# Small fp32 products in places of the array, and the inverse moved out of the chain, in a one-layer gMLP and RWKV-7 step

## The chip, the core and the metric

The kernel runs on one core of one Trainium2 chip, in one launch. The metric is device time in microseconds (us). An execution before the change took 1997.01 us (median of three, 1996.12 to 1997.17).

## The reference

One layer of a hybrid trunk takes 1024 prompt frames and 64 sample frames of width 2048, in fp32. Its core, cut:

```
z = rms_norm(x) @ w_in                       # 2048 -> 7296 columns
u, v, g_a | r, k, v_b, hw, ha | g_b = z      # the second group is token-shifted
out_a = gelu(u) * (tril(W_s) @ layer_norm(gelu(v)) + b_s) * silu(g_a)
w = exp(-exp(-softplus(-(w0 + tanh(hw) @ w2)) - 0.5));  a = sigmoid(a0 + ha @ a2)
kk = normalise_per_head(k * k_k);  k = k * (1 + (a - 1) * k_a)
for each t:                                  # 16 heads of 64, state S is 64 x 64
    S = S * w_t + (-S @ kk_t) (kk_t * a_t)^T + v_t k_t^T
    y_t = S @ r_t
out_b = (group_norm(y) + (r.k.r_k per head) * v) * silu(g_b)
y = rms_norm(x + [out_a ; out_b] @ w_out)
```

## The kernel before, in words

**Projections.** Both large products run in f16. Each fp32 operand is split by a power-of-two scale into a high and a low half, and three passes (high by high, high by low, low by high) stand for one fp32 product. The input projection is cut into 57 blocks of 128 columns. Each block runs over three groups of frames (364, 364 and 360), with 16 k-tiles of three passes in each. These products write the tile mp from the h operands, which lie in `big` (bigt in the profile), and the weight halves w. The out-projection is cut into two halves of the mixed columns, and within each into eight groups of 256 output columns; it reads the mixed operands from mixT. Operand j of a half is a tile of 128 columns by 1088 frames. `mix_stage` (L1169) reads it from DRAM into a buffer, and `mix_prep` (L1131) makes its high half on ACT and its low half on DVE. `out_first` (L1203) is the first group: for a tile of 128 frames it runs over operands 0 to 5 first, then 6 and 7. In the kernel before, the first three operands are placed in the tile hw and two buffers of the keys, and the other five in u buffers as these come free.

**The RWKV part.** It runs beside the input projection and the first out-projection half, one pair of heads q at a time, in 16 chunks of 64 frames plus the sample's chunk 16. For each pair:

- `front(q)` (L771) makes decay, a, the normalised keys and the scaled operands AR (from kk and r) and KB (from b and k). It sums squares over each head with a 128x128 block matrix of ones, `bones`, and it does so again for the bonus.
- `wkv(q)` (L867) makes the masked products of each chunk in MK: MA (for the delta rule) and MR (for the output). The side generator `ktr` transposes KB for the state update. Then it inverts a unit triangular matrix per chunk and head: 32x32 blocks by DVE steps, and the block between them by two batches of 32x32 products on TensorE (L953 to L971).
- MA holds two blocks per chunk and head: the inverse, and the block that multiplies the values. The products L982 to L991 apply the second to the values; POOL then clears it, so that what is left of MA is the inverse of both heads on its diagonal.
- The chain (L996 to L1048) then goes from chunk to chunk: a product of AR with the state S into yps, the sum with the values into `sar` on DVE, the product of the inverse with sar (L1006), two copies of the result into VS, the product of the transposed keys with VS, and the new state on DVE. After every fourth chunk, four products of MR with VS give the output y.

**What sets the order.** The program text emits one instruction list, in the order in which a planner in Python runs. `mm` (L221) adds an estimate to the clock of TensorE. Every two or three f16 products, `poll` (L151) lets each waiting side generator whose time has come emit its next piece. So the fp32 products stand between f16 products, where the planner expects their inputs to be there. A piece that emits several products without a `yield` puts them directly one behind another. Small products write PSUM tiles from two pools with two buffers each: `bigt` (bigp in the profile) and `smt` (smp). A product that reuses a buffer waits until the buffer's reader, mostly ACT, is through.

Engines are named as in the profile: PE is TensorE, ACT is ScalarE, DVE is VectorE, POOL is GpSimd, SP issues DMAs.

## Time and profile before

| | |
|---|---|
| median of three runs | 1997.01 us |
| profiled execution, its own time | 1997.49 us |
| span of its instructions | 1995.4 us |
| PE busy | 1948.3 us, 98% |
| DVE busy | 1295.7 us, 65% |
| ACT busy | 967.5 us, 48% |
| POOL busy | 351.4 us, 18% |
| mean granted clock of TensorE | 0.993 |
| HBM traffic | 91 GB/s over the span |

Busy time of an engine is the time in which it has an instruction under way. Products on TensorE are pipelined, and the end of one is modelled, so its duration runs into the start of the next; the time from one start to the next is what a product takes from the engine. An fp32 product shows as two instructions. The span leaves out about 2 us around the first and last instruction, which the execution's time holds.

### The profile page before, as it was taken

Reading aid. Unit: us, or ns where it says so; the run is one execution under the profiler, and the core shown is the slowest. Engines: PE = TensorE matmul, PEld = TensorE weight load, DVE = VectorE, ACT = ScalarE, POOL = GpSimd, SP = SyncE. Lnnn points to the kernel's source line nnn. Section 1 sums busy time; section 2 is a strip of 40 time slices with the busy share of each in tenths; the row PEclk is TensorE's granted clock in tenths of the full one; section 3 lists DMA queues with packets and bytes.
Section 4 is the critical chain, followed back from the end, with each engine's and each line's share of the span. In section 5 each row is a group of like instructions: output and inputs, shape, how many; then the busy total and the mean of one; then the engine's idle time right before and its main releaser. Section 6 shows DMA issues by size and latency. Waiting matters only on the chain. (4 is left out here: it accounts for less than half of the span.)

```text
span 1995.4 us, 40192 instructions
## 1 busy us (share of the span) xinstructions
PE 1948.3 (98%) x16709; PEld 1421.8 (71%) x16709; DVE 1295.7 (65%) x3173; ACT 967.5 (48%) x1702; POOL 351.4 (18%) x352
## 2 busy tenths in 40 slices
PE   6999999999999999999999999999999899999998
PEld 6966667656766666676676677667667578889997
DVE  6584684494686667667667765956766686663444
ACT  7642352536455544744555564374465524242433
POOL 2500002500420330041023023004202401000000
PEclk8999999999999999999999999999999999999999
DMA  6221114121212212312321231222222353142114
GB/s 237 86 75 43 46 66 171 67 76 70 88 63 99 85 58 77 122 56 80 100 100 48 77 123 58 77 92 87 79 90 99 144 193 109 35 156 97 74 43 139
DMA packets 49301, 183.79 MB, mean 92 GB/s; under 512 B 6560, under 2 KB 18352, under 8 KB 39456
## 3 DMA queue, kind: packets, MB, share of 16 engines
q1 hardware_dynamic: 39792, 150.02, 21.0%
q0 software_dynamic: 6880, 22.26, 3.2%
q10 hardware_dynamic: 2448, 8.94, 1.1%
q8 instruction: 132, 2.16, 0.4%
q14 instruction: 49, 0.40, 0.1%
HBM read 135.86 MB, written 45.38 MB: 91 GB/s over the span
## 5 line engine op out<-in xcount | busy, mean ns | idle before, releaser
L231 PE MATMUL mp<-bigt,w 128*128 128x364 f16 (+3 forms) x8496 | 1337.7, 310 | 2.2 <-DVE w L190 1.4
L231 PEld LDWEIGHTS <-w 128*128 128x128 f16 x9216 | 821.1, 99 | 409.0 <-issue 16.3
L190 DVE SCALAR_TENSOR_TENSOR w<-raw,sci,w 128x512 f16<-128x512 f32 x276 | 220.6, 814 | 87.7 <-ACT w L182 86.0
L231 PEld LDWEIGHTS <-wk 128*128 128x128 f16 x2304 | 210.0, 98 | 28.9 <-DVE wk L190 4.8
L182 ACT ACTIVATE w<-raw,sci 128x512 f16<-128x512 f32 x276 | 186.3, 713 | 68.2 <-DVE sci L268 65.1
L231 PE MATMUL mp<-w,wk 128*128 128x256 f16 x1728 | 205.6, 273 | 4.2 <-DVE wk L190 4.2
L194 POOL TENSOR_TENSOR u<-u,u 128x1088 f32<-128x1088 f32 x56 | 138.0, 2475 | 288.1 <-DVE u L190 207.1
L182 ACT ACTIVATE w<-raw 128x2048 bf16<-128x2048 f32 (+1 forms) x70 | 131.8, 1883 | 81.2 <-PE mp L231 76.5
L182 ACT ACTIVATE wk<-bigp 128x512 f32<-128x512 f32 (+5 forms) x200 | 94.3, 492 | 123.0 <-PE bigp L231 88.9
L214 DVE STREAM_TRANSPOSE wk<-u 32x288 f32<-32x288 f32 (+1 forms) x256 | 115.8, 452 | 52.0 <-ACT u L182 47.5
L182 ACT ACTIVATE u<-mp,sc 128x364 f32<-128x364 f32 (+3 forms) x109 | 57.1, 524 | 183.8 <-PE mp L231 182.8
L231 PE MATMUL mp<-w,u 128*128 128x256 f16 x960 | 122.6, 275 | 6.7 <-DVE u L190 6.7
L182 ACT ACTIVATE u<-mp,zs 128x364 f32<-128x364 f32 (+1 forms) x75 | 42.0, 560 | 166.9 <-PE mp L231 162.5
L182 ACT ACT_TABLE_LOAD x91 | 116.8, 1283 | 9.9 <-PE bigp L231 6.0
L190 DVE SCALAR_TENSOR_TENSOR S<-S,pc,smp 64x64 f32<-64x64 f32 x240 | 66.9, 279 | 70.0 <-PE smp L231 68.1
L190 DVE SCALAR_TENSOR_TENSOR bigt<-mp,sc,bigt 128x512 f32<-128x512 f32 (+2 forms) x83 | 54.0, 652 | 86.9 <-PE mp L231 86.4
L231 PEld LDWEIGHTS <-u 128*128 128x128 f16 x960 | 94.0, 99 | 20.1 <-DVE u L190 8.0
L990 POOL MEMSET wk<- 64x512 f32 (+1 forms) x48 | 18.9, 395 | 500.2 <-PE bigp L231 498.7
L194 POOL TENSOR_TENSOR wk<-wk,mask 128x512 f32<-128x512 f32 (+1 forms) x80 | 83.1, 1058 | 130.5 <-ACT wk L182 119.8
L182 ACT ACTIVATE u<-yps 64x128 f32<-64x128 f32 x120 | 32.7, 272 | 143.0 <-DVE sar L194 134.4
L231 PE MATMUL bigp<-wk 64*128 64x128 f32 (+2 forms) x1360 | 99.6, 259 | 0.0
L231 PEld LDWEIGHTS bigp<-wk 64*128 64x128 f32 (+2 forms) x1360 | 85.3, 167 | 18.9 <-issue 9.4
(179 smaller groups left out, 2087.9 us busy)
## 6 DMA issues: line engine op xcount, KB each, us to landing
raw<-w_in SPq DMA_DIRECT2D x54, 1024.0 KB, 4.8
raw<-w_out SPq DMA_DIRECT2D x14, 1024.0 KB, 4.9
z_d<-u SPq DMA_DIRECT2D x24, 544.0 KB, 2.9
u<-z_d SPq DMA_DIRECT2D x24, 544.0 KB, 5.5
mix_d<-u ACTq DMA_DIRECT2D x16, 544.0 KB, 2.7
u<-mix_d POOLq DMA_DIRECT2D x16, 544.0 KB, 5.5
o_y<-bigt SPq DMA_DIRECT2D x16, 512.0 KB, 4.0
wk<-x SPq DMA_DIRECT2D x7, 1024.0 KB, 7.7
```

The source lines that it names most:

```text
L182: self.nc.scalar.activation(out, in_, func, bias=bias, scale=scale, **kw)
L190: self.nc.vector.scalar_tensor_tensor(out, in0, s, in1, op0, op1)
L194: (eng or self.nc.vector).tensor_tensor(out, a, b, op)
L214: self.nc.vector.transpose(out, a)
L231: self.nc.tensor.matmul(out, lhsT, rhs, start=start, stop=stop)
L990: nc.gpsimd.memset(MA[hp, c0:c0 + m, g, :], 0.0)
```

## The change

**In places of the array.** Head sums are made by `head_sums`: four products of 64x64 ones blocks, each in its own quarter of the array, for 1024 frames, and two for the last 64. The two batches of 32x32 products spread the chunks over four column places. The y products become sixteen of 128x64 for eight chunks at a time, where they were four of 128x128 for four chunks.

**The inverse outside the chain.** A new side generator `atr` transposes A per chunk. `products` runs twice, where the kernel before has one set of products with the values. Between its two runs, the transposed A is multiplied by MA and written back into AR, so that the chain's first product already carries the inverse. The chain's own product with the inverse goes, with its tile `sar`, its two copies and the memsets of MA on POOL.

**Operands in the input buffer.** Operands 0 and 1 of the first out-projection half go to the two key buffers. The others go to u buffers if there is room while the input projection runs, and otherwise into the input buffer `big` once its last products are emitted. `mix_move` later copies these into u buffers by SP's queue, and the loads of x into the same buffer wait for it. The tile hw moves to DRAM and is read back for each pair; that makes room for a 13th u buffer.

**The planner.** A side generator is passed over while DVE's clock is more than its backlog ahead; the allowance for a hand-over in the chain (slack) goes from 200 to 100 ns; some products get a stated cost.

```diff
-    def add(self, gen, front=False):
+    def add(self, gen, front=False, backlog=600):
         if front:
-            self.side.insert(0, [0, gen])
+            self.side.insert(0, [0, gen, 1e9])
         else:
-            self.side.append([0, gen])
+            self.side.append([0, gen, backlog])
 
     def poll(self):
         self.npoll += 1
         assert self.npoll < 60000, [(g.__name__, g.gi_frame.f_lineno) for _, g in self.side]
         for it in list(self.side):
-            if it[0] > self.now:
+            if it[0] > self.now or self.clk[DV] > self.now + it[2]:
                 continue
...
+    def head_sums(self, a, b=None):
+        b = a if b is None else b
+        pa, pb, ps = self.bigt(), self.bigt(), self.smt()
+        for h in range(2):
+            hp, br, one = HP[h], HP[1 - h], self.bones[HP[h], HP[h]]
+            self.mm(pa[hp, :], one, a[hp, 0:512], cost=260)
+            self.mm(pb[br, :], one, a[hp, 512:1024], cost=260)
+        for hp in HP:
+            self.mm(ps[hp, 0:64], self.bones[hp, hp], a[hp, NP:NT], cost=55)
+        parts = [(slice(0, 128), slice(0, 512), pa[:])] + [(HP[h], slice(512, 1024), pb[HP[1 - h]]) for h in range(2)]
+        parts.append((slice(0, 128), slice(NP, NT), ps[:, 0:64]))
+        return [(a[p, c], i) if b is a else (a[p, c], i, b[p, c]) for p, c, i in parts]
...
-        for t0, n in TG:
-            pt = self.bigt()
-            self.mm(pt[:, 0:n], self.bones[:], R[:, t0:t0 + n])
-            f = self.tt(V[:, t0:t0 + n], pt[:, 0:n], V[:, t0:t0 + n], ALU.mult)
-            yield f - 300
+        for _, i, o in self.head_sums(R, V):
+            f = self.tt(o, i, o, ALU.mult)
+        yield f
...
-        slack = 200 if q < 7 else 0
+        slack = 100 if q < 7 else 0
...
+        def atr():
+            ti = P["at"] = yield from self.galloc()
+            At = self.u[ti][:, 0:NT].rearrange("p (c f) -> p c f", f=64)
+            for c0, m in ((0, 8), (8, 8), (16, 1)):
+                pt = self.bigt()
+                for c in range(c0, c0 + m):
+                    for hp, br, g in hs:
+                        self.mm(pt[br, (c - c0) * 64:(c - c0) * 64 + 64], AR[hp, c, 0, :], self.ident[hp, hp], cost=55)
+                f = self.act(At[:, c0:c0 + m], pt[:, 0:m * 64].rearrange("p (c f) -> p c f", f=64), AF.Copy)
+                yield f + 300
+            self.flags.add(("at", q))
+        hs = [(HP[0], HP[1], 1), (HP[1], HP[0], 0)]
         for part, (c0, c1) in enumerate(PARTS):
             yield from self.wait(("ark", q, part))
-            self.add(vtr(part))
+            self.add(vtr(part), backlog=1500)
...
-            self.add(ktr(part))
+            self.add(ktr(part), backlog=1e9)
         yield fm - 300
+        self.add(atr(), backlog=1e9)
...
-        for c0, m in ((0, 16), (16, 1)):
-            pt = self.bigt()
-            for c in range(c0, c0 + m):
-                for p0, g in HEADS:
-                    self.mm(pt[p0 + 32:p0 + 64, (c - c0) * 32:(c - c0) * 32 + 32], MA[p0:p0 + 32, c, g, 32:64],
-                            Q1[p0:p0 + 32, c, :])
+        pt = self.bigt()
+        for c in range(NCH):
             for p0, g in HEADS:
-                z = slice(p0 + 32, p0 + 64)
-                f = self.act(PT[z, c0:c0 + m, :], pt[z, 0:m * 32].rearrange("p (e s) -> p e s", s=32), AF.Copy)
+                o = p0 + 32 * (1 - c % 2)
+                self.mm(pt[o:o + 32, c // 2 * 32:c // 2 * 32 + 32], MA[p0:p0 + 32, c, g, 32:64], Q1[p0:p0 + 32, c, :],
+                        cost=22)
+        ev = lambda o, n: pt[o:o + 32, 0:n * 32].rearrange("p (e s) -> p e s", s=32)
+        for p0, g in HEADS:
+            z = slice(p0 + 32, p0 + 64)
+            self.act(PT[z, 0:NCH:2, :], ev(p0 + 32, 9), AF.Copy)
+            f = self.act(PT[z, 1:NCH:2, :], ev(p0, 8), AF.Copy)
...
-        flat = lambda ap: ap.rearrange("p g k -> p (g k)")
-        hs = [(HP[0], HP[1], 1), (HP[1], HP[0], 0)]
-        for c0, m in ((16, 1), (0, 8), (8, 8)):
+        yield from self.wait(("at", q))
+        At = self.u[P["at"]][:, 0:NT].rearrange("p (c f) -> p c f", f=64)
+        def products(src):
+            pt = self.smt()
+            for hp, br, g in hs:
+                self.mm(pt[br, 0:64], MA[src(hp, br), 16, g, :], VS[src(hp, br), 16, hp], cost=55)
+            for hp, br, g in hs:
+                self.act(VS[br, 16, hp], pt[br, 0:64], AF.Copy)
+            pts = [self.bigt() for _ in range(2)]
+            for c in range(16):
+                for hp, br, g in hs:
+                    self.mm(pts[c % 2][(br, hp)[c % 2], c // 2 * 64:c // 2 * 64 + 64], MA[src(hp, br), c, g, :],
+                            VS[src(hp, br), c, hp], cost=30)
+            for i in range(2):
+                for hp, br, g in hs:
+                    f = self.act(VS[br, i:16:2, hp], pts[i][(br, hp)[i], :].rearrange("p (c f) -> p c f", f=64), AF.Copy)
+            return f
+        fk = products(lambda hp, br: hp)
+        for c0, m in ((0, 8), (8, 8), (16, 1)):
             pt = self.bigt()
             for c in range(c0, c0 + m):
                 for hp, br, g in hs:
-                    self.mm(pt[br, (c - c0) * 64:(c - c0) * 64 + 64], MA[hp, c, g, :], VS[hp, c, hp])
-            for hp, br, g in hs:
-                f = self.act(VS[br, c0:c0 + m, hp], pt[br, 0:m * 64].rearrange("p (c f) -> p c f", f=64), AF.Copy)
-            for hp, br, g in hs:
-                nc.gpsimd.memset(MA[hp, c0:c0 + m, g, :], 0.0)
-            yield f - 300
+                    self.mm(pt[hp, (c - c0) * 64:(c - c0) * 64 + 64], At[br, c], MA[br, c, g, :], cost=55)
+            f = self.act(AR[:, c0:c0 + m, 0, :], pt[:, 0:m * 64].rearrange("p (c f) -> p c f", f=64), AF.Copy)
+        yield max(fk, f - 2000)
+        f = products(lambda hp, br: br)
+        self.free(P["at"])
         nc.gpsimd.memset(Y[0:64, 0, :], 0.0)
         yield from self.wait(("kbfree", q))
...
-            for hp, br, g in hs:
-                if Sc is None:
-                    f = self.copy(self.sar[br], VS[br, c, hp])
-                else:
-                    f = self.tt(self.sar[br], px[0:64, hp], VS[br, c, hp], ALU.add)
-            yield f + slack
-            pb = self.smt()
-            self.mm(pb[:, 0:64], flat(MA[:, c]), self.sar[:])
-            for hp, br, g in hs:
-                f = self.copy(VS[br, c, hp], pb[br, 0:64])
-            if Sc is not None:
+                for hp, br, g in hs:
+                    f = self.tt(VS[br, c, hp], px[0:64, hp], VS[br, c, hp], ALU.add)
+                yield f + slack
                 self.act(yd, px[64:128, 0:128], AF.Copy)
-            yield f + slack
             pu = self.smt()
             self.mm(pu[:, 0:128], KBt[:, c], VS[:, c])
             Sn = self.S[c % 2 if c < 16 else 1]
@@ -1022,19 +1060,21 @@
                     f = self.stt(Sn[hp, hp], Sc[hp, hp], pc[hp, c - 1:c], pu[hp, hp], ALU.mult, ALU.add)
                 else:
                     f = self.copy(Sn[hp, hp], pu[hp, hp])
-            if c == 16 or c % 4 == 3:
-                cs = [16] if c == 16 else range(c - 3, c + 1)
+            if c == 16:
                 pt = self.bigt()
-                for r, d in enumerate(cs):
-                    self.mm(pt[:, r * 128:(r + 1) * 128], flat(MR[:, d]), VS[:, d])
+                self.mm(pt[:, 0:128], MR[:, c].rearrange("p g k -> p (g k)"), VS[:, c])
                 for hp, br, g in hs:
-                    if c == 16:
-                        self.tt(yd[:, hp], pt[br, hp], yd[:, hp], ALU.add)
-                        continue
-                    pv = pt[br, :].rearrange("p (i j f) -> p i j f", j=2, f=128)
+                    self.tt(yd[:, hp], pt[br, hp], yd[:, hp], ALU.add)
+            elif c % 8 == 7:
+                pt = self.bigt()
+                for r in range(8):
+                    for hp, br, g in hs:
+                        self.mm(pt[br, r * 64:r * 64 + 64], MR[:, c - 7 + r, g, :], VS[:, c - 7 + r, hp], cost=65)
+                for hp, br, g in hs:
+                    pv = pt[br, :].rearrange("p (i j f) -> p i j f", j=2, f=64)
                     for j in range(2):
-                        y = Y[j * 64:j * 64 + 64, c // 2 - 1:c // 2 + 1, hp]
-                        self.tt(y, pv[:, :, j, hp], y, ALU.add)
+                        y = Y[j * 64:j * 64 + 64, c // 2 - 3:c // 2 + 1, hp]
+                        self.tt(y, pv[:, :, j, :], y, ALU.add)
...
         if half == 0:
-            yield from self.wait(("ark", 7))
-        self.add(self.mix_stage(half))
+            yield from self.wait(("kbfree", 7))
+        self.add(self.mix_stage(half), backlog=1e9)
...
+    def mix_place(self, j):
+        while "inproj" not in self.flags:
+            if self.room7():
+                self.mixA.append(self.alloc())
+                return self.U(self.mixA[-1]).bitcast(F16)
+            yield
+        self.mixB.append(j)
+        o = 8192 + (len(self.mixB) - 1) * NT
+        return self.big[:, o:o + NT].bitcast(F16)
+
     def mix_stage(self, half):
+        nb = 0
         for j in range(8):
-            while len(self.mstg) >= 2:
+            while len(self.mstg) >= (3 if half or "inproj" not in self.flags else 5):
...
+            if stg is None:
+                R = self.big[:, 2048 + nb % 5 * NT:2048 + nb % 5 * NT + NT]
+                nb += 1
+            else:
+                R = self.U(stg)
+            self.mstg[half, j] = (stg, R, self.dma(self.nc.gpsimd, R, self.mix_d[HALF[half][j]], 1 << 19))
...
+    def mix_move(self):
+        yield from self.wait(("mixT", 0))
+        mt = self.mixT[0]
+        for n, j in enumerate(self.mixB):
+            while not self.room7():
+                yield
+            i = self.alloc()
+            self.mixA.append(i)
+            d, o = self.U(i).bitcast(F16), 8192 + n * NT
+            yield self.dma(self.nc.sync, self.U(i), self.big[:, o:o + NT], 1 << 19)
+            mt[j] = (d[:, 0:NT], d[:, NT:2 * NT])
+        self.flags.add("moved")
...
                 if b == 31:
-                    self.add(self.mix_prep(0, None))
+                    self.add(self.mix_prep(0, None), backlog=1e9)
+                if jobs[i + 1][0] == "out":
+                    self.flags.add("inproj")
+                    self.add(self.mix_move(), backlog=1e9)
```

How the order moves, at three places. The first is PE at the products with the values in the first head pair. In these rows wk is the arena that holds MA, VS and AR, u2 the transposed A, mp the f16 product; the number behind a name tells buffers' uses apart. Before, a batch stands between f16 products:

```order
L231 LDWEIGHTS w00_76
L231 MATMUL mp_4810<-bigt_74,w00_76 128x364
L231 MATMUL bigp_4829<-wk_80 64x64 x16
L231 LDWEIGHTS w00_76
L231 MATMUL mp_4810<-bigt_74,w00_76 128x364
```

After:

```order
L232 MATMUL bigp_4820<-wk_80 64x64 x2
L232 MATMUL bigp_4821<-wk_80 64x64 x2
L232 MATMUL bigp_4858<-wk_80,u2_83 64x64 x16
L232 MATMUL bigp_4876<-wk_80,u2_83 64x64 x16
L232 MATMUL bigp_4894<-wk_80,u2_83 64x64 x2
L232 LDWEIGHTS w10_78
L232 MATMUL mp_4804<-bigt_74,w10_78 128x360
```

The products of 64x64 now follow one another, from the last chunk products into two PSUM tiles (4820 and 4821) to the A products into the next three, and only then comes an f16 product.

The second place is PE at the chunk products of a later pair (bigp<-wk of 128x128) and the key transposes (bigp<-ident,wk). Before:

```order
L231 MATMUL mp<-bigt,w_78 128x364
L231 MATMUL bigp<-wk 128x128 x8
L231 LDWEIGHTS w_79
L231 MATMUL mp<-bigt,w_79 128x364
L231 LDWEIGHTS w_78
L231 MATMUL mp<-bigt,w_78 128x364
```

After:

```order
L232 LDWEIGHTS w_77
L232 MATMUL mp<-bigt,w_77 128x364
L232 MATMUL bigp<-wk 128x128 x8
L237 MATMUL bigp<-ident,wk 128x128 x4
L232 LDWEIGHTS w_76
L232 MATMUL mp<-bigt,w_76 128x364
```

The key transposes now stand directly behind a batch of chunk products, with f16 products behind both.

The third place is DVE where the input projection hands over to the out-projection. The low halves are the rows of 128x544 with pwi; the rows of u with u alone are steps of the last pair's inverse, and STREAM_TRANSPOSE is its preparation. Before:

```order
L214 STREAM_TRANSPOSE wk<-u_89 32x9x32
L190 SCALAR_TENSOR_TENSOR wk<-u_81,pwi,wk 128x544
L214 STREAM_TRANSPOSE u_85<-wk 32x1024
L190 SCALAR_TENSOR_TENSOR wk<-u_90,pwi,wk 128x544
L202 TENSOR_SCALAR sc_113<-sci_116,pwi 128x1
L190 SCALAR_TENSOR_TENSOR wk<-u_90,pwi,wk 128x544
L214 STREAM_TRANSPOSE wk<-u_89 32x9x32
L190 SCALAR_TENSOR_TENSOR u_92<-u_86,pwi,u_92 128x544
L214 STREAM_TRANSPOSE u_85<-wk 32x1024
L190 SCALAR_TENSOR_TENSOR u_92<-u_86,pwi,u_92 128x544
```

After:

```order
L189 SCALAR_TENSOR_TENSOR u_88<-bigt,pwi,u_88 128x544
L193 TENSOR_TENSOR u_87<-u_92 128x150
L193 TENSOR_TENSOR u_92<-u_92,u_87 128x6x25
L193 TENSOR_TENSOR u_87<-u_92 128x130
L193 TENSOR_TENSOR u_92<-u_92,u_87 128x5x26
L189 SCALAR_TENSOR_TENSOR u_88<-bigt,pwi,u_88 128x544
L268 TENSOR_SCALAR sci_116<-smp 128x1
L269 TENSOR_SCALAR sci_116<-sci_116 128x1
L273 TENSOR_SCALAR sci_116<-sci_116 128x1
L189 SCALAR_TENSOR_TENSOR bigt<-bigt,pwi 128x544
L193 TENSOR_TENSOR u_87<-u_92 128x108
```

Among the low halves there now stand steps of the inverse where there were transposes before, and the source of the low halves is the input buffer bigt in place of a u buffer.

## Rows read from the trace of the kernel before

**Rows 1.** The page: span, and busy time, share and instructions of each engine.
```profile
span 1995.4 us, 40192 instructions
PE 1948.3 (98%) x16709; PEld 1421.8 (71%) x16709; DVE 1295.7 (65%) x3173; ACT 967.5 (48%) x1702; POOL 351.4 (18%) x352
```

**Rows 2.** Windows: stretch, its us, busy us (instructions) by engine, clock, DMA, GB/s.
```profile
300.00:1550.00 1250.00, 1239.56 (x9742) 844.28 (x9740) 840.38 (x2196) 652.56 (x1101) 273.47 (x251) 1.00 0.24 85
...
1585.00:1605.00 20.00, 9.06 (x43) 4.79 (x41) 19.53 (x29) 11.67 (x17) 6.56 (x9) 0.66 0.79 284
```

**Rows 3.** Groups by form, TensorE: operands, array tile, shape, count, busy us, mean ns.
```profile
L231 PE MATMUL smp<-sar,wk 128*128 128x64 f32 x272 | 46.3, 252 | 1.7 <-DVE sar L194 1.7
...
L231 PE MATMUL bigp<-wk 128*128 128x128 f32 x272 | 36.9, 275 | 0.0
...
L231 PE MATMUL bigp<-u,bones 128*128 128x512 f32 x64 | 33.8, 610 | 0.0
...
L231 PE MATMUL bigp<-wk 64*64 64x64 f32 x544 | 21.0, 223 | 0.0
...
L231 PE MATMUL bigp<-wk,u 32*32 32x32 f32 x544 | 10.1, 192 | 0.0
```

**Rows 4.** Timeline, TensorE: start, us, line, operands, tile, shape, count.
```profile
626.91 0.33 PE L231 MATMUL bigp<-wk 64*64 64x64 f32 x4
627.17 1.41 PE L231 MATMUL mp<-bigt,w 128*128 128x364 f16 x8
628.51 1.15 PE L231 MATMUL bigp<-wk 64*64 64x64 f32 x32
629.59 1.72 PE L231 MATMUL mp<-bigt,w 128*128 128x364 f16 x10
631.14 0.17 PE L231 MATMUL smp<-sc,ones 128*128 128x1 bf16 x1
```

**Rows 5.** Timeline, TensorE: the chain's product with the inverse.
```profile
654.46 0.33 PE L231 MATMUL smp<-sar,wk 128*128 128x64 f32 x2
654.63 0.32 PE L231 MATMUL mp<-bigt,w 128*128 128x360 f16 x1
```

**Rows 6.** Timeline, TensorE: a batch of four y products.
```profile
719.20 1.06 PE L231 MATMUL bigp<-wk 128*128 128x128 f32 x8
720.10 0.32 PE L231 MATMUL mp<-bigt,w 128*128 128x364 f16 x1
```

**Rows 7.** Timeline, TensorE: a batch of 34 products of 32x32.
```profile
620.03 1.26 PE L231 MATMUL bigp<-u,wk 32*32 32x32 f32 x68
621.23 0.33 PE L231 MATMUL mp<-bigt,w 128*128 128x360 f16 x1
```

**Rows 8.** Timeline, TensorE: a head-sum product, and f16 steps of 256 columns.
```profile
1607.34 1.02 PE L231 MATMUL bigp<-u,bones 128*128 128x512 f32 x2
1608.20 0.71 PE L231 MATMUL mp<-w,wk 128*128 128x256 f16 x5
1608.75 0.49 PE L231 MATMUL mp<-w,u 128*128 128x256 f16 x3
```

**Rows 9.** Groups by form, ACT: eviction of one half of a PSUM bank.
```profile
L182 ACT ACTIVATE wk<-bigp 64x512 f32<-64x512 f32 x32 | 18.9, 591 | 12.1 <-PE bigp L231 11.5
```

**Rows 10.** Timeline, TensorE: key transposes of the first pair.
```profile
385.91 0.33 PE L236 MATMUL bigp<-ident,wk 128*128 128x128 f32 x1 [0.55 <-ACT wk L182]
```

**Rows 11.** Waits of TensorE: releaser, us in total, times, longest.
```profile
PE mp L231 <- DVE u L190: 6.7, 3, 2.9
PE mp L231 <- DVE wk L190: 4.2, 2, 3.6
...
PE smp L231 <- DVE wk L210: 2.9, 4, 1.8
```

**Rows 12.** The page: DMA reads of the mixed operands, us from issue to landing.
```profile
u<-mix_d POOLq DMA_DIRECT2D x16, 544.0 KB, 5.5
```

**Rows 13.** Groups by form, DVE: low halves of the mixed operands.
```profile
L190 DVE SCALAR_TENSOR_TENSOR wk<-u,pwi,wk 128x544 f16<-128x544 f32 x20 | 14.9, 776 | 1.1 <-ACT wk L182 1.0
```

155 lines of the change are left out of this document (82 added, 73 removed).

## The prediction

> **What bounds the kernel now.** The page comes first: TensorE is busy for 1948.3 of 1995.4 us [rows 1], so a change is worth what it takes from TensorE's own work, plus what it takes from or adds to the 47 us in which TensorE waits. The windows by stretch come second. In the long middle, where the eight head pairs run between the f16 products, TensorE idles 1250.00 − 1239.56 = 10.4 us; in the 20 us where the input projection hands over to the out-projection it works 9.06 us, at a granted clock of 0.66 [rows 2]. The groups by form say how often each small fp32 product runs [rows 3]; an fp32 product is two instructions there. Their busy times overlap, so prices come from the timeline: from a batch's start to the next f16 product's start [rows 4 to 8]. The profiled execution took 1997.49 us, 0.5 above the median of the runs; the sum is made against it, and 0.2% of it, 4 us, is what a measurement can tell from no change.
>
> **Prices.** Ten f16 steps take 631.14 − 629.59 = 1.55 us, 0.155 each. Eight of them ahead of a batch of 64x64 products take 628.51 − 627.17 = 1.34, 0.10 more than 1.24: the way into the other tile shape. Sixteen products then take 629.59 − 628.51 = 1.08 us and two take 627.17 − 626.91 = 0.26 [rows 4]. So one product more costs 0.82/14 = 59 ns, a batch costs 0.24 us beside its products (0.14 of it behind the switch-in), and a batch of 16 costs 1.18, of two 0.36. The two heads of such a pair of products stand in different rows and different columns of the array, and 59 ns each is what that overlap leaves.
>
> **Removed.** The chain's product with the inverse: 272/2 = 136 at 0.17 [rows 3, 5] = 23.1 us. The y products: 32 batches of four at 0.90 [rows 6] = 28.8. Head sums: 32 at 0.86 [rows 8] = 27.5, and 16 of 64 columns, which I price like the 0.17 of [rows 5], = 2.7. Inverse times kV: eight pairs at 2 × 1.18 + 0.36 = 21.8. The 32x32 batches: 16 at 1.20 + 0.10 [rows 7] = 20.8. Together 124.7 us.
>
> **Added.** Transposes of A: again 2.72 per pair = 21.8. First products and A products, which run on in one row: 0.24 + 2 × 0.059 + 32 × 0.029 + 34 × 0.059 = 3.29 per pair = 26.3; second products 0.24 + 0.12 + 0.94 = 1.30 = 10.4. y products 16 × 1.18 = 18.9. Head sums: four quarters side by side 0.86, plus 0.24 and 0.12 for the 64 columns, 1.22 × 16 = 19.5. 32x32 over four column places: between 0.78 and the old 1.30; I take 0.90 × 16 = 14.4. Together 111.3, so TensorE's work falls by 13 us.
>
> The prices 0.029, 1.18 for y and 0.86 for four quarters assume that two products in the same rows but in different columns overlap. No row of before shows that pair alone. Without it the chunks of both products run at 59 (32 × 0.030 × 16 = 15 us more), the y products at twice 59 (15 more), the head sums at 2 × 0.86 (14 more), and the 32x32 as before (6 more): 50 us. I take the overlap, because the row- and column-distinct pair already runs at half of one pass, and keep the other end as a rival. The Trainium skill (TensorEngine Tiling (Array Packing), Tiling Modes) calls the four 64x64 places independent; [rows 4] bears that out for two of the four, and by the page the sum would be the −13 above.
>
> **Waits that come in.** In the new order the A products follow the first products with no f16 product between them, and their two buffers are those the products have just filled. TensorE waits until ACT has emptied the first: two evictions of 64x512 at 591 ns [rows 9] = 1.18 us, plus the hand-off and less the 0.14 of switching that passes meanwhile, about 1.2. Behind it on TensorE stands everything, f16 products included. Eight pairs 9.6; in the first two the ACT queue holds weight conversions and a table load ahead, 0.8 more each: 11.2 us (0 if f16 products could come between, 20 if ACT is always late). The Trainium skill (TensorEngine Tiling (Array Packing), Performance Considerations, PSUM Bottleneck) has the rule that speaks against the change: tiling speeds TensorE but not the copies out of PSUM. By that rule the 0.94 us of a four-place batch against the 2.4 us that its four evictions take would cost the difference, 1.4 per pair and 12 in all, close to the 11 above.
>
> A low-rank product follows the second products nearly at once in five pairs and needs one of their buffers: an eviction of 0.59 us, five times, 3 us (0 to 6). The transposes of the keys now may run whatever DVE's backlog, and stand directly behind a batch of chunk products in every pair; before, this happened in the first pair alone and left 0.55 us of idle time [rows 10]. Seven more pairs: 3.9 us (0 to 8). In the chain the planner's allowance falls from 200 to 100 ns. TensorE's waits for the chain's copies were 2.9 us [rows 11] with the longer allowance; I take 2 us more (0 to 5; the two copies that vanish from each link work the other way).
>
> **Waits that go.** The first out-projection group needs operands 0 to 5 before it can go on. TensorE waited 6.7 + 4.2 = 10.9 us there for DVE's low halves [rows 11], until 16 us after the last input product. Now operands 2 to 5 are read into the input buffer when the last input group ends: 5.5 us for a read [rows 12], 0.7 for the high half on ACT, then eight low halves at 0.776 [rows 13] = 6.2, with some 1.2 us of inverse steps between them in DVE's new order: 13.6 us. So I take −2 (+5 if these five reads and the weight reads slow each other, −13 if DVE has nothing else). The copies into u by SP's queue and the x loads behind them have to be there only when the first group is through: 64 tile steps of three products each, at (1608.75 − 1608.20)/5 = 0.11 us [rows 8], 21 us. They hide behind those; without that cover one copy would cost up to the 5.5 us of a read.
>
> DVE loses two copies and half the y sums per link, POOL 48 memsets, and a side generator is now passed over while DVE is behind. The 10.4 us of idle middle [rows 2] are mostly TensorE coming to a chain product before DVE. I take −6 (0 to −10).
>
> **Sum.** −13 + 11.2 + 3 + 3.9 + 2 − 2 − 6 = −1, and 1997.5 − 1 = 1996 us: no change that can be measured, because the work that goes comes back as waits for ACT.
>
> **Rivals.** *The hand-over heals.* If DVE's queue is short there, the idle time falls from 10.9 us to some 2, and 9 of the gain come: 1987. For it: the new DVE order shows mostly short inverse steps among the low halves where before 1.9 us transposes stood. Against it: 5.5 us of reading is now behind the last input product, where before it was ahead of it.
>
> *The columns do not overlap.* One mechanism, in the array: two products that share rows run one after the other. Price 50 us, 2046 in full; it decides as soon as a tenth of it holds, since −1 + 5 is over the bound. For it: no row shows the overlap. Against it: the 59 ns.
>
> *The clock falls.* The clock was granted at 0.66 of its 2.4 GHz in the hand-over, where TensorE waited [rows 2], that is at 1.2 GHz for part of it. If a wait of 1.2 us inside 4 us of small products brings it down in each pair, these 3.3 us take twice as long: 8 × 3 = 24, 2020. Against it: the idle spots in the middle left that stretch's clock at 1.00 [rows 2].
>
> *The buffer waits are larger.* Each pair's key transposes wait 1.1 us, and the chain's shorter allowance costs its 5: 7 × 0.55 + 3 = 7 more, 2003. For it: the pattern is in every pair's order. Against it: ACT is busy less than half the time.
>
> **How the numbers follow.** The sum's case has a chance of 0.52, on its own 1989 to 2004, split 0.18 faster, 0.27 same, 0.07 slower. Hand-over 0.24, faster. Columns 0.07, clock 0.06, larger buffer waits 0.11, all slower. So faster 0.42, same 0.27, slower 0.31. The range reaches from below the healed hand-over, with some of the idle middle gone too, to beyond the larger waits: 1983 to 2014; the columns and the clock stay outside.
>
> **What would show it.** A batch of 32 chunk products that lasts 0.9 to 1.0 us shows the overlap, 1.9 refutes it. A products with 1.2 us of idle time ahead and ACT's eviction as the releaser show the wait; if the middle's idle time stands at 10 us or less, I am wrong there. Waits for DVE around the first out-projection products of 8 to 10 us confirm that term, 3 or fewer the first rival. The forecast falls if the small products' work shrinks by much more than 13 us.

## The result: 2.7% slower, and the time is in waits

The changed kernel takes 2050.74 us (median of 4 runs, 2046.09 to 2053.95) where the kernel before takes 1996.57 (4 runs, 1994.78 to 1997.17): a ratio of 1.0271, with a 95% interval of 1.0249 to 1.0293. The forecast was 1996 within 1983 to 2014; it was wrong, and its range was too short. The profiled execution took 2053.95 us, 56.5 above the one before; it is the longest of the four.

The page of the changed kernel, in answer to [rows 1]:

```profile
span 2052.2 us, 43339 instructions
PE 1961.4 (96%) x18421; PEld 1412.0 (69%) x18421; DVE 1256.1 (61%) x2829; ACT 1029.5 (50%) x1817; POOL 342.2 (17%) x304
```

TensorE's idle time went from 47.1 to 2052.2 − 1961.4 = 90.8 us. The windows say where (columns as in [rows 2]; the second stretch is the hand-over, which stands later now):

```profile
300.00:1550.00 1250.00, 1211.13 (x11010) 809.65 (x11008) 803.81 (x1896) 703.79 (x1194) 260.62 (x208) 0.99 0.25 87
...
1630.00:1670.00 40.00, 17.92 (x177) 12.48 (x176) 29.61 (x54) 15.65 (x25) 4.72 (x5) 0.69 0.55 202
```

The middle, which idled 10.4 us, now idles 38.9; the hand-over idles 22 us of 40. The products themselves are as cheap as forecast. The changed kernel's timeline of TensorE shows, from above, an A-product batch behind its wait, a batch of 16 y products, a set of head sums, a 32x32 batch and the second products:

```profile
458.00 2.50 PE L232 MATMUL bigp<-wk,u 64*64 64x64 f32 x68 [2.54 <-ACT wk L181]
460.43 2.92 PE L232 MATMUL mp<-bigt,w 128*128 128x360 f16 x18
...
503.38 1.15 PE L232 MATMUL bigp<-wk 128*64 128x64 f32 x32
504.46 0.48 PE L232 MATMUL mp<-bigt,w 128*128 128x364 f16 x2
...
561.32 1.09 PE L232 MATMUL bigp<-u,bones 64*64 64x512 f32 x8
562.23 0.29 PE L232 MATMUL smp<-u,bones 64*64 64x64 f32 x4
562.45 0.64 PE L232 MATMUL mp<-bigt,w 128*128 128x364 f16 x3
...
1657.65 0.79 PE L232 MATMUL bigp<-u,wk 32*32 32x32 f32 x68
1658.37 0.39 PE L232 MATMUL mp<-w,bigt 128*128 128x256 f16 x2
...
1682.61 0.27 PE L232 MATMUL smp<-wk 64*64 64x64 f32 x2
...
1682.74 1.13 PE L232 MATMUL bigp<-wk 64*64 64x64 f32 x62
1683.81 0.39 PE L232 MATMUL mp<-w,wk 128*128 128x256 f16 x2
```

Read start to start: 16 y products 1.08 us, head sums with their last 64 columns 1.13, a 32x32 batch 0.72 [rows 7: 1.20], second products 1.20. With about 0.10 for the way in, these are 1.18, 1.23, 0.82 and 1.30; the prediction had 1.18, 1.22, 0.90 and 1.30.

What TensorE waits for, by releaser (us in total, times, longest), in answer to [rows 11]:

```profile
PE bigp L232 <- ACT wk L181: 20.8, 15, 2.5
PE mp L232 <- DVE bigt L189: 19.9, 5, 9.6
...
PE smp L232 <- DVE wk L193: 7.5, 7, 2.6
PE bigp L237 <- ACT wk L181: 5.5, 12, 0.7
```

To see every loss, the short ones too, the table below counts TensorE's time from the start of each instruction to the start of the next, by kind of product, over the whole input projection; idle time stands with the product that ended it, and an f16 product counts with its usual step. It is worked out from the starts in the four traces. "Buffers" is `e15_keys_smt` and "same order" is `e10_same_order`, two kernels of the experiments below.

```
us up to the last input product      before  changed  buffers  same order
inverse product in the chain           23.5      0        0       29.0
y products                             26.6     17.3     17.1     19.2
head sums                              29.0     20.3     20.3     23.1
32x32                                  18.1     12.5     12.4     11.8
transposes of A                           0     21.7     21.6      0
A products                                0     32.1     14.7      0
64x64 products with kV                 18.9     20.0     17.4     18.9
chain: products with S                 26.9     36.2     39.4     29.1
chain: products with the keys          32.1     38.8     40.5     38.0
chunk products                         42.7     48.4     43.3     42.8
key and other transposes               54.4     60.6     51.7     54.2
low-rank products                      18.9     21.2     19.7     22.9
f16 products above their usual step     7.9     13.5     10.0      8.7
all, with f16 and the rest           1581.4   1626.5   1593.6   1580.7
behind the last input product         401.8    413.3    397.0    399.4
```

Of the 56.6 us, 45.1 arise in the input projection and 11.5 behind it.

### The profile page after: what moved, and what is told of

The parts are those of the page before. It is cut to its first block, busy times and chain, and to the rows that moved or that the text cites. A ratio compares the mean times of both kernels' runs of the same rounds, so it can differ in the third digit from the quotient of the medians.

```text
span 2052.2 us, 43339 instructions
## 1 busy us (share of the span) xinstructions
PE 1961.4 (96%) x18421; PEld 1412.0 (69%) x18421; DVE 1256.1 (61%) x2829; ACT 1029.5 (50%) x1817; POOL 342.2 (17%) x304
## 3 DMA queue, kind: packets, MB, share of 16 engines
q1 hardware_dynamic: 42960, 157.82, 21.7%
## 4 chain that ended last, share of the span: by engine, by line
PE 86%; DVE 5%; ACT 5%; DMA 2%; issue 1%; SPq 0%; DVEq 0%; ACTq 0%
PE mp L232 73%; PE bigp L232 8%; ACT wk L181 2%; DVE u L193 2%; PE smp L232 2%; PE bigp L237 2%; PE yps L232 2%; ACT u L181 1%; DMA o_ss<-S 1%; DMA u<-bv_d 1%; DVE w L189 1%; DVE u L189 1%; DMA bigt<-x 1%; ACT L181 0%; DVE bigt L189 0%
## 5 line engine op out<-in xcount | busy, mean ns | idle before, releaser
L189 DVE SCALAR_TENSOR_TENSOR w<-raw,sci,w 128x512 f16<-128x512 f32 x276 | 217.8, 812 | 170.9 <-ACT w L181 169.7
L232 PE MATMUL mp<-w,wk 128*128 128x256 f16 x1728 | 205.9, 275 | 12.3 <-DVE bigt L189 12.3
L181 ACT ACTIVATE wk<-bigp 128x512 f32<-128x512 f32 (+3 forms) x240 | 120.3, 521 | 78.3 <-PE bigp L232 55.0
L181 ACT ACT_TABLE_LOAD x102 | 130.9, 1283 | 52.6 <-PE bigp L232 17.6
L213 DVE STREAM_TRANSPOSE wk<-u 32x256 f32<-32x256 f32 (+1 forms) x256 | 115.6, 451 | 51.2 <-ACT u L181 43.6
L232 PE MATMUL mp<-w,u 128*128 128x256 f16 x1053 | 131.1, 275 | 2.9 <-DVE u L189 2.5
L232 PEld LDWEIGHTS <-u 128*128 128x128 f16 x1053 | 103.2, 99 | 18.0 <-DVE u L189 2.7
L189 DVE SCALAR_TENSOR_TENSOR u<-mp,zs,u 128x363 f32<-128x363 f32 (+1 forms) x100 | 49.4, 494 | 88.7 <-ACT sht L181 67.0
L193 DVE TENSOR_TENSOR u<-u,u 128x30 f32<-128x30 f32 (+15 forms) x248 | 92.5, 373 | 8.2
L193 DVE TENSOR_TENSOR u<-u 128x30 f32<-128x30 f32 (+14 forms) x240 | 92.3, 385 | 5.9
L232 PE MATMUL bigp<-wk 64*64 64x64 f32 (+2 forms) x2096 | 86.7, 240 | 3.3 <-ACT wk L181 1.8
```

The source lines that it names most:

```text
L181: self.nc.scalar.activation(out, in_, func, bias=bias, scale=scale, **kw)
L189: self.nc.vector.scalar_tensor_tensor(out, in0, s, in1, op0, op1)
L193: (eng or self.nc.vector).tensor_tensor(out, a, b, op)
L213: self.nc.vector.transpose(out, a)
L232: self.nc.tensor.matmul(out, lhsT, rhs, start=start, stop=stop)
```

## The experiments

Ratios are to the kernel before, run on the same chip, with 95% intervals. Two theories stood at first, and the expectations name them: W, the time is lost in waits of TensorE (for the buffers that ACT empties, in the chain, whose allowance fell from 200 to 100 ns, at one late read of x, and by the clock); P, the small products cost more on the array than they save. The table already speaks against P.

**The read of x for the output sums.** After the hand-over the changed kernel's TensorE and DVE stand still once for 9.6 us. Its timeline of SP's queue, of TensorE and of DVE:

```profile
1643.71 1.95 SPq L240 DMA_DIRECT2D u<-bigt  x2
1656.46 0.33 SPq L240 DMA_DIRECT2D raw<-w_out  x1
1656.85 0.43 SPq L240 DMA_DIRECT2D bigt<-x  x1
```

```profile
1668.38 1.44 PE L232 MATMUL mp<-w,wk 128*128 128x256 f16 x6 [9.62 <-DVE bigt L189]
```

```profile
1667.58 1.41 DVE L189 SCALAR_TENSOR_TENSOR bigt<-mp,sc,bigt 128x512 f32<-128x512 f32 x2 [9.65 <-DMA bigt<-x]
```

DVE cannot add a finished product to x because x is not there; its read was issued 26.7 us behind the last input product (at 1630.2). Before, it went out at 1579.75, ahead of the last input product. The read is a side generator of the planner (`acc_load`), and by the new default every such generator is passed over while DVE's planned queue is more than 600 ns behind. The planner holds this first read back for nothing else: of the reads of x, only the later ones wait for the copies out of the input buffer (L1333 to L1336 of the changed kernel). `e2_xload` exempts the generator:

```diff
-        self.add(self.acc_load())
+        self.add(self.acc_load(), backlog=1e9)
```

> The changed kernel; only the generator that reads x for the out-projection's sums is no longer passed over when DVE is behind, so that its read stands ahead of the copies of operands and of a weight read in SP's queue. Theory W: the wait of 9.6 us of TensorE in the first out-projection group goes, 2038 to 2043, and nothing changes before the hand-over. Rival P, or a wait that is taken by the next late operand: 2047 to 2055.

Measured: 2031.44 us, 1.0172 [1.0156, 1.0187], below both ranges. The read goes out at 1617.18, as this row of SP's queue in that kernel shows, and the wait is gone:

```profile
1617.18 0.38 SPq L240 DMA_DIRECT2D bigt<-x  x1
```

TensorE's idle time behind 1550 us is 23.2 instead of 36.6 us. That is 13.4 of the 24.0 us by which the two profiled executions differ (2053.95 and 2029.95; the medians differ by 19.3). Another 6.7 us lie ahead of the last input product, where the order of TensorE's products and the idle time of the middle (39.0 and 38.9 us) are the same: there TensorE spent 34 us at half the clock in the changed kernel's profile and 14 in this one. The late read is shown as a cause, of some 13 us.

**The chain's allowance** (`e1_slack200`):

```diff
-        slack = 100 if q < 7 else 0
+        slack = 200 if q < 7 else 0
```

> The changed kernel with the chain's allowance (slack) back at 200 ns. Theory W (the time is lost in waits of TensorE that the new order makes: evictions by ACT between first products and A products 17 us, chain products that come before DVE is through 16 us, key transposes and chunk products behind ACT 12 us, the late read of x 12 us, the clock 6 us): up to the hand-over the chain's products with S and with the keys cost 8 to 14 us less, so 2034 to 2043; the read of x also stands earlier in SP's queue here and may take off another 8. Rival P (the small products in column places and the inverse outside the chain cost more on the array than they save): the allowance changes nothing, 2047 to 2055.

Measured: 2057.29 us, 1.0299 [1.0284, 1.0314]: 6.5 slower than the changed kernel, not faster, and outside both ranges. What W put down to the allowance (8 to 14 us) falls. But the edit moved more than the chain: the waits for the chain's S rose to 10.3 us in 7 places.

**Distance between the products** (`e3_spread`) lets the planner place f16 products between the first, A and second products:

```diff
         fk = products(lambda hp, br: hp)
+        yield fk + 300
...
-        yield max(fk, f - 2000)
+            yield f + 300
         f = products(lambda hp, br: br)
+        yield f + 300
```

> The changed kernel, with a pause of the generator behind the first products, behind each batch of A products and behind the second products, so that f16 products stand where TensorE waited for ACT. Theory W: the A products fall from 4.6 us per pair to some 2.3 and the idle time ahead of them goes, 12 to 17 us less, 2033 to 2040. Rival P: the same products cost the same wherever they stand, 2046 to 2055.

Measured: 2055.45 us, 1.0295 [1.0277, 1.0312]: at the upper end of P's range, but not for P's reason. Its waits by releaser:

```profile
PE yps L232 <- DVE S L189: 15.9, 12, 4.3
...
PE bigp L232 <- ACT wk L181: 5.3, 5, 2.1
```

The wait for ACT fell as expected, and the A products cost 18.9 us in place of 32.1; the chain's products with S rose from 36.2 to 49.7. What was gained at one place was lost at another, and each `yield` makes the planner lay out everything behind it anew. From here on, either the order was kept and only a buffer changed, or the redrawn order was itself the object.

**Other buffers, same order.** `e5_ypool` has the early read and writes the first and second products to the chain's pool, so that the A products find free buffers:

```diff
-            pts = [self.bigt() for _ in range(2)]
+            pts = [self.ps_y.tile([128, 512], F32, tag="y", name="yps") for _ in range(2)]
```

> e2_xload with the first and second products written to the two PSUM buffers of the chain's first product (idle between chains) in place of the pool that the A products use. The order up to the hand-over is that of e2_xload, 2031. Theory W: the idle time ahead of the A products (14 us over the pairs) and part of the waits inside them and ahead of the low-rank products go: 2011 to 2020. Rival M (a wait that is taken away comes back at the next link, because the chain's products are emitted before DVE is through, as in e3_spread): 2026 to 2033.

Measured: 2027.59 us, 1.0157 [1.0142, 1.0172], only 4 less than with the early read alone, in the range of the rival. The timeline of its TensorE, and of its ACT, at the first pair:

```profile
454.10 2.03 PE L232 MATMUL bigp<-wk,u 64*64 64x64 f32 x64
458.67 0.45 PE L232 MATMUL bigp<-wk,u 64*64 64x64 f32 x4 [2.54 <-ACT wk L181]
```

```profile
455.07 0.46 ACT L181 ACTIVATE wk<-smp 64x64 f32<-64x64 f32 x2
455.56 2.44 ACT L181 ACTIVATE wk<-yps 64x512 f32<-64x512 f32 x4
458.02 1.36 ACT L181 ACTIVATE wk<-bigp 128x512 f32<-128x512 f32 x3
```

The first two A batches start without a wait; the third needs a buffer of the first, which ACT reaches only behind the four evictions of the first products, 0.61 us each. The wait moved on by 64 instructions and kept its 2.54 us. `e13_third_smt` gives that third batch (one chunk) the small pool:

```diff
-            pt = self.bigt()
+            pt = self.bigt() if m > 1 else self.smt()
```

> e5_ypool with the third batch of A products (the sample's chunk) written to the pool of small tiles. In e5_ypool the wait of 1.3 to 2.5 us per pair had moved from the first batch of A products to the third, behind ACT's four evictions. Theory W: it goes now, 2012 to 2019. Rival M (it comes back elsewhere): 2025 to 2030.

Measured: 2015.32 us, 1.0091 [1.0077, 1.0105], 12 less, as W said. The timeline of TensorE at the same place:

```profile
452.42 2.03 PE L232 MATMUL bigp<-wk,u 64*64 64x64 f32 x64
454.29 0.28 PE L232 MATMUL smp<-wk,u 64*64 64x64 f32 x4
454.50 2.92 PE L232 MATMUL mp<-bigt,w 128*128 128x360 f16 x18
```

First products, A products and f16 products now run on without a gap. `e15_keys_smt` does the same for the key transposes, which stand directly behind chunk products:

```diff
-                pt = self.bigt()
+                pt = self.smt()
```

> e13_third_smt (2015) with the key transposes written to the pool of small tiles, so that they no longer share two buffers with the chunk products. Same order. Theory W: TensorE's waits for ACT at the key transposes (5.4 us), and as much that stretches the chunk products beside them, go: 2004 to 2010. Rival M (they come back at the next link of the chain): 2013 to 2017.

Measured: 2004.19 us (7 runs), 1.0032 [1.002, 1.0043], 11 less, again as W said. In the column "buffers" of the table the A products cost 14.7 us instead of 32.1, and transposes and chunk products, 109.0 in the changed kernel, 95.0. From 2031.44 to 2004.19 the three edits take back 27 us, and in the traces of these kernels TensorE, ACT and DVE run the same instructions in the same order: PSUM buffers that ACT had not emptied are shown as the largest cause. With the read of x, four small edits give back some 46 of the 54 us between the medians (ratio 1.0271 to 1.0032). The Trainium skill (TensorEngine Tiling (Array Packing), Performance Considerations, PSUM Bottleneck) says that tiling speeds up TensorE but not the copies out of PSUM, which may then become the bottleneck; the trace agrees, with 2.54 us of waiting ahead of 2.50 us of products. Its advice to share the copies with the vector engine was not tried here.

**One part alone** (`e4_places`): the kernel before with only the products in places of the array (head sums, y, 32x32), the planner laying out the order anew.

```diff
-        for t0, n in TG:
-            pt = self.bigt()
-            self.mm(pt[:, 0:n], self.bones[:], SQ[:, t0:t0 + n])
-            f = self.act(SQ[:, t0:t0 + n], pt[:, 0:n], AF.Ln)
-            yield f - 300
+        for o, i in self.head_sums(SQ):
+            f = self.act(o, i, AF.Ln)
+        yield f - 300
...
```

> The kernel before with only the places of the array: head sums in four quarters, 32x32 products over four column places, y products as sixteen of 128x64 for eight chunks. The inverse stays in the chain, the planner and the out-projection's operands are those of before. Theory W: the y products save 9.9 us, the head sums 10, the 32x32 batches 7, no new wait: 1968 to 1976. Rival P: not below the kernel before, 1993 or more.

Measured: 2050.34 us, 1.0269 [1.0254, 1.0284], 53 slower than before and in P's range. Windows of its last input stretch and the two behind it:

```profile
1500.00:1550.00 50.00, 49.39 (x503) 32.64 (x501) 36.20 (x86) 32.29 (x49) 6.48 (x13) 1.00 0.29 99
1550.00:1600.00 50.00, 27.27 (x124) 18.55 (x122) 25.18 (x83) 21.77 (x35) 12.47 (x6) 0.58 0.24 88
1600.00:1650.00 50.00, 29.23 (x150) 20.96 (x149) 28.27 (x58) 19.09 (x34) 20.92 (x23) 0.50 0.20 68
```

The input ends at 1549.5, some 35 us earlier than before, and then TensorE runs out of f16 products while the last pair is still in DVE's and ACT's hands: 43 us idle in 100, at a granted clock near 0.5, its level of 1.2 GHz. The f16 products are cover; spent too soon, they are missing at the end. In the kernel before, the last pair's chunk products begin behind the 8690th of the 8832 f16 products ahead of the out-projection, here behind the last of them.

`e6_places_fast` lets side work in after every f16 product, with the shorter allowance; `e7_before_fast` does the same to the kernel before, without the places.

```diff
-        per = 2 if n > 256 else 3
+        per = 1
...
-        slack = 200 if q < 7 else 0
+        slack = 100 if q < 7 else 0
```

> e4_places (kernel before with the column places alone) with side work polled after every f16 product in place of every second, and a slack of 100 ns. In e4_places the input projection was 33 us ahead at 1550 us, but the last pair's keys came after the last input product, and TensorE waited for the chain. Here they come 280 f16 products before it. Theory C (the places save what they should, and the loss of e4_places is the pace of the chain): 1970 to 1982. Rival: the faster pace costs TensorE as much in waits for DVE, 1993 or more.

> The kernel before with the polling after every f16 product and the slack of 100 ns alone: the control for e6_places_fast. Theory C: no work goes, more chain products start before DVE is through, 1997 to 2008. Rival (the polling itself is the gain): under 1990.

Measured: 2022.71 us, 1.013 [1.0115, 1.0145], with the places; 2050.75, 1.027 [1.0253, 1.0287], without. At the faster pace the places gain 28 us, about what the prediction's prices for these three kinds say (28.8 − 18.9 + 30.2 − 19.5 + 20.8 − 14.4 = 27.0). But the two kernels also differ in order, so the agreement may be luck. The pace itself costs the kernel before 54 us without any change of its work, where 0 to 11 were expected: e7's idle time in the middle is 40.7 us. So the order of the kernel before is one of many that its planner could give, and a favourable one among those tried.

`e8_inverse_back` takes the changed kernel with the early read and the faster pace, and puts the inverse back into the chain:

```diff
+            pb = self.smt()
+            self.mm(pb[:, 0:64], flat(MA[:, c]), self.sar[:])
+            for hp, br, g in hs:
+                f = self.copy(VS[br, c, hp], pb[br, 0:64])
...
```

> The changed kernel with the early read of x, polling after every f16 product, and the inverse back in the chain as before (no transposes of A, no A products, no second products; sar and the copies again). Theory W: the inverse outside the chain costs 14 us of work and some 17 of waits for ACT; without it and with the places, 1975 to 1992. Rival (the planner's backlog rule and the operands in the input buffer are what costs): 2015 or more.

Measured: 2040.63 us, 1.0217 [1.0202, 1.0232]. That is in the rival's range, but its largest wait is of the same kind as e7's (15.1 us for the chain's copies, 12.2 in e7), so it shows the pace again and says nothing clear on the inverse or on the rival.

**Two other draws of the kernel before**, `e12_draw210` and `e14_draw250`, differ from it in one number of the planner's and in no operation:

```diff
-        slack = 200 if q < 7 else 0
+        slack = 210 if q < 7 else 0
```

(250 in the second.)

> The kernel before with a slack of 210 ns in place of 200: no work changes, the planner lays another order at a third of the places on DVE. Theory D (the order of before is one that was picked; any other order of the same work has more waits): 2003 to 2035. Rival (orders are alike, a longer allowance takes waits away): 1993 to 1999.

> The kernel before with a slack of 250 ns: a second other order of the same work. Theory D: 2003 to 2035. Rival: 1993 to 2000.

Measured: 2012.93 us, 1.008 [1.0065, 1.0096], and 2000.38 (10 runs), 1.0016 [1.0007, 1.0025]; the second misses theory D's range. A redraw alone moves this kernel by 3 to 16 us, as much as the 13 us that the whole sum turned on.

**The places in the order of before.** `e10_same_order` is e4 with the planner's clocks advanced by the old estimates, and with the y products in groups of four chunks as before, so that the side operations keep their places:

```diff
+        ck, fn = list(self.clk), self.func
         for o, i in self.head_sums(SQ):
-            f = self.act(o, i, AF.Ln)
-        yield f - 300
+            self.act(o, i, AF.Ln)
+        self.clk = ck
+        for t0, n in TG:
+            self.clk[PE] += max(n, 128) * 4 / 2.4 + 7
...
```

> The kernel before with head sums in four quarters, 32x32 products over four column places and y products as eight of 128x64 for four chunks, while the planner's clocks are advanced by the old products' estimates: its order stays that of before apart from the places themselves. Theory O (the places save what they should; the loss of e4_places is that shorter estimates make the planner lay another order): y 6, head sums 10, 32x32 7 us less and no new wait, 1970 to 1980. Rival: the places bring waits whatever the order, 1993 or more.

Measured: 1993.81 us (11 runs), 0.9984 [0.9975, 0.9993], the fastest kernel that does all of the work, and within the rival's range. Counted by the f16 products ahead of them, the chain's products stand where they stood, but for 11 or 12 of the 136 links between 840 and 895 us, which moved by up to 18 f16 products; these account for 0.9 us of the idle time. The products of these kinds became 19.6 us cheaper in the input projection (last column of the table: 7.4 + 5.9 + 6.3), and the time up to the last input product fell by 0.7. The chain and the low-rank products took it back: 5.5 + 2.2 + 5.9 + 4.0 = 17.6. The waits of this kernel's middle, 300 to 1550 us, where idle time rose from 10.4 to 25.2:

```profile
PE smp L231 <- DVE sar L194: 5.2, 7, 1.5
PE smp L231 <- DVE wk L210: 5.1, 8, 1.8
PE bigp L231 <- DVE lwh L190: 3.9, 3, 1.6
PE yps L231 <- DVE S L190: 3.0, 2, 1.7
```

One of them in the timeline of all engines:

```profile
666.62 1.32 ACT L182 ACTIVATE w<-raw,sci 128x512 f16<-128x512 f32 x2
667.36 0.75 DVE L190 SCALAR_TENSOR_TENSOR w<-raw,sci,w 128x512 f16<-128x512 f32 x1 [2.87 <-ACT w L182]
...
668.03 0.57 DVE L190 SCALAR_TENSOR_TENSOR S<-S,pc,smp 64x64 f32<-64x64 f32 x2
...
668.66 0.49 PE L231 MATMUL yps<-S,wk 128*128 128x128 f32 x2 [1.66 <-DVE S L190]
```

DVE stands 2.87 us at a weight's low half, whose high half ACT has not converted yet; the chain's S is queued behind it on DVE, and the next product of the chain waits for S. TensorE came there earlier because its products were shorter; ACT and DVE did not. Five chain products in this middle come right behind a low half that stood 2.9 to 5.3 us for ACT: 6.7 of the 13.3 us that TensorE idles ahead of the chain's products there, and none of the five waited over 0.1 us in the kernel before.

`e16_no_yadd` asks whether the y sums in DVE's queue are the load: e10 without them (it leaves out adding the y products to the output; the planner still counts them).

```diff
-                        self.tt(y, pv[:, :, j, :], y, ALU.add)
+                        self.fin(DV, 150 + 128 / 0.96)
```

> e10_same_order (1994) without the 128 DVE sums that add the y products to the output of chunks 0 to 15, which this kernel leaves out; the planner's clocks still count them, so the order stays. They stand in DVE's queue directly ahead of the next link's sums. Theory Q (with the order fixed, the 22 us that the places save come back at chain products that wait for DVE's queue, so DVE's queue has to get shorter too): 1978 to 1988. Rival L (the link's own latency holds the chain, whatever DVE has queued): 1990 to 1996.

Measured: 1989.9 us, 0.9966 [0.9953, 0.9979], 4 less and just below rival L's range. Its waits for the chain are those of e10 to a few tenths (5.8, 5.2 and 3.0 us in the same rows), and counted as in the table the 4 us stand at the head sums (23.1 to 19.1). So the number of DVE's operations is not what holds the chain; that it is what single operations in DVE's queue wait for is read from the trace, and no run took those waits away.

## Why the prediction was wrong

**Its step that failed** is the one on the waits that go and the chain: the idle middle is "mostly TensorE coming to a chain product before DVE. I take −6", with "2 us more" for the chain's allowance. Together −4. The chain's two products rose by 9.3 + 6.7 = 16.0 us in the input projection alone. The thought behind it was that a chain with fewer copies on DVE waits less. But the planner laid the whole kernel out anew, and it plans by estimates: the order of before was a favourable draw among those tried, and the changed one need not be. The redraws (3 to 54 us with no work changed) show that a loss of this size can come that way; that this draw accounts for the chain's 16 us is inferred, since the inverse part alone in a kept order was not run. e10 shows another way to the same loss: with the order nearly kept and the inverse still in the chain, the chain's three products rose by 13.6 us, because TensorE came to them earlier. How the 16 us split between the two stays open.

The trace of the changed kernel does say what DVE stood at. Of the 10.8 us that TensorE idles at the chain's products in the middle, 8.2 go back, along DVE's queue, to an operation on the input projection's results (u<-mp) that stood 0.5 to 3.8 us for ACT. The largest, on DVE and on TensorE:

```profile
1516.32 0.52 DVE L189 SCALAR_TENSOR_TENSOR u<-mp,zs,u 128x295 f32<-128x295 f32 x1 [3.78 <-ACT sht L181]
```

```profile
1517.84 0.46 PE L232 MATMUL smp<-wk 128*128 128x128 f32 x2 [2.62 <-DVE wk L193]
```

**The hand-over: −2 was forecast.** The waits for operands are 2.45 + 2.12 + 4.12 + 1.41 = 10.1 us in the changed timeline around 1636 to 1647, against 10.9 before, 0.8 less: the 8 to 10 us that the text gave as a sign came. What it passed over is the x read. It said that x loads behind the copies "have to be there only when the first group is through" and hide behind 21 us of tile steps; but DVE came to the first sums at about 1658, the read was issued at 1656.85, and 12.3 us of waits for the sums followed. The sums are also wanted earlier than that sentence says: `out_first` adds a pair of tiles as soon as its eight operands are through (L1285), not behind the group. The step counted a DMA's cover from its place in the queue, not from when the planner lets it in; the passed-over side generators were named among the gains (−6) and not among the costs.

**Waits for ACT: 11.2 for the A products.** Measured 32.1 − 14.7 = 17.4 in seven pairs, inside the 0 to 20 that was given, with 2.54 us in the first pair for a forecast of 2.0. The mechanism was right. Its price was too low for what stands ahead on ACT. The changed kernel's ACT at the first pair:

```profile
455.51 0.56 ACT L181 ACTIVATE u<-mp,zs 128x364 f32<-128x364 f32 x1
455.97 0.25 ACT L181 ACTIVATE zc<-mp,sc 128x1 f32<-128x1 f32 x1
456.25 0.46 ACT L181 ACTIVATE wk<-smp 64x64 f32<-64x64 f32 x2
456.74 3.06 ACT L181 ACTIVATE wk<-bigp 64x512 f32<-64x512 f32 x5
```

The first products end by 455.45. ACT has two operations of the f16 side ahead, 0.8 us, then empties the two single chunks in 0.5, and only then needs the 1.2 us that were priced. The sum had the 0.8 in two pairs, and the 0.5 in none.

**Key transposes: 3.9 forecast,** 6.2 measured, and 5.7 more at the chunk products in front of them, which want the same buffers; e15 takes both away. **Low-rank: 3 forecast,** 2.3 measured.

**The work: right.** In the whole execution the removed kinds fell by 26.8 (inverse), 10.7 (y), 11.5 (head sums) and 6.6 us (32x32), against 21.7 for the transposes of A and, without their waits as in e15, 19.8 for the A products: −14. With the products with the values, 1.0 dearer, it is the −13 that was forecast. That two products in the same rows and different columns overlap is shown by the y batch at 1.08 us, where the rival without overlap had twice 59 ns for each of the 16; that rival is refuted.

**The rivals.** The case of larger buffer waits had the right mechanism and sign, with 7 us on top of the sum's 18; 31.6 came (17.4 + 2.3 + 6.2 + 5.7). The falling clock came in places: after two waits of 1.0 and 1.2 us an A batch ran 3.49 us instead of 2.50 in the changed kernel:

```profile
608.87 1.15 PE L232 MATMUL bigp<-wk 64*64 64x64 f32 x60 [1.03 <-ACT u L181]
611.25 3.49 PE L232 MATMUL bigp<-wk,u 64*64 64x64 f32 x68 [1.22 <-ACT wk L181]
```

```profile
605.00:610.00 5.00, 3.97 (x92) 2.61 (x82) 0.80 (x3) 4.11 (x10) 0.20 (x1) 1.00 0.08 28
610.00:615.00 5.00, 3.51 (x70) 3.45 (x69) 0.00 (x0) 3.28 (x6) 0.00 (x0) 0.66 0.01 3
```

The clock of that window was 0.66, and the mean of the profiled execution fell from 0.993 to 0.983. Behind the last input product the time at half the clock fell from 37 to 21 us when e2 took the late read away. Ahead of it, it fell from 34 to 14 although the waits of the middle stayed, so part of it differs between executions. The hand-over did not heal. Two of the rivals' sums were off: with the text's own terms the healed hand-over gives −13 + 11.2 + 3 + 3.9 + 2 − 9 − 6 = −8, which is 1989 and not 1987, and 8 × 3.3 us for the clock is 26 and not 24.

**The range** took each wait with its own bounds and none for a new order of everything. All of the waits but the low-rank products' missed to the same side.

**What stays open.** With buffers and the read mended, e15 is still 8 us slower than before although its products are cheaper; the chain's two products are 12.5 and 8.4 us longer than before there. Of some 14 us that TensorE idles at the chain's products in its middle, 8.8 go back to DVE standing for ACT at an operation on the input projection's results, as above. Another 4.7, in five places, are a wait that the kernel before does not have: a new state is written into the tile that the store of the sample's state, `o_ss`, is still reading. DVE stands there for 7.4 us in e15, for 3.7 in the changed kernel and for none before:

```profile
1123.13 0.59 DVE L189 SCALAR_TENSOR_TENSOR S<-S,pc,smp 64x64 f32<-64x64 f32 x2 [2.17 <-DMA o_ss<-S]
```

No run took either away, so what that would give is open.

## What to carry to other kernels

Where a planner sets the order, price the redraw first: change one neutral number, time it, and take that spread as the floor of what a saving must beat; or keep the old order by feeding the planner the old estimates. When small products get faster, look at once at who empties their buffers, and follow that in-order engine to the next buffer that it holds: freeing one may only move the wait, as in e5. A busy share of 98% does not mean that work taken off that engine is gained; here 20 us less of it gave 3, because the engines beside it were only tenths of a microsecond ahead: in the kernel before, half of the chain's products started less than 0.35 us behind DVE's last write of their operand.

## What the runs showed of the hardware

- Four places of 64x64 run together: 32 fp32 chunk products and two single ones take 1.20 us from start to start, 34 A products over two places 2.1 (452.42 to 454.50 in e13). The Trainium skill (TensorEngine Tiling (Array Packing), Tiling Modes) calls the places independent; the trace agrees.
- DVE's idle time ahead of the weights' low halves, 169.7 us of it for ACT, is nearly double in the changed kernel. The group of its page:

```profile
L189 DVE SCALAR_TENSOR_TENSOR w<-raw,sci,w 128x512 f16<-128x512 f32 x276 | 217.8, 812 | 170.9 <-ACT w L181 169.7
```

  Before it was 87.7. An engine that is idle 39% of the time can still hold up a chain, because its queue stops at the first operation that is not ready, as the rows of e10 at 667.36 show.
- Idle spots of 1 to 1.2 us on TensorE were followed by a stretch at half the clock in one place, and spots of 1.3 to 2.5 us by none in others (the A batch at 458.00 took 2.50 us); what decides it was not settled.
